# A planner that counts ScalarE's function-table loads and prices scans anew, in a hybrid encoder step on one core

## The chip, the cores and the metric

The kernel runs on one core of one Trainium2 chip. The metric is the device time of one execution in microseconds (us), the median of several runs. The engines are named as the profile names them: PE is TensorE's matmul, PEld its weight load, DVE is VectorE, ACT is ScalarE, POOL is GpSimd, SP is SyncE, which issues all DMA transfers here.

## What is computed

One layer of a streaming encoder, for a prompt of 2048 frames and for 32 frames of a running stream with 1024 cached positions. The reference, cut to what matters:

```python
xn = rmsnorm(x, g_mix)                       # model width 1024
q, k, v, u, gate = split(xn @ w_in)          # 5 x 512 columns
q, k = head_rmsnorm(q), head_rmsnorm(k)      # 8 heads of 64
# stick-breaking attention, s < t only:
z = q @ k.T / 8
sp = where(mask, softplus(z), 0)
log_a = log_sigmoid(z) - (reverse_cumsum(sp) - sp)
o = where(mask, exp(log_a), 0) @ v
# convolution branch
c = causal_dwconv(u * sigmoid(gate), 31 taps)
c = silu(layernorm(c))
h = x + concat([o, c]) @ w_out
up = causal_dwconv(rmsnorm(h) @ w_up, 3 taps)    # 5632 columns
a, g = split(up)
y = h + (silu(g) * a) @ w_down
```

## The kernel before

All matrix products run in a split form: a value is kept as a high and a low part (the helper split, line 579: an ACT copy makes the high part, a DVE subtraction the low one), and each product is three matmuls. Phase 1 (line 851) makes the projections of w_in in two halves of the prompt. Then four feed-forward blocks of 512 frames follow (feed, line 1213): for each of 22 column tiles two up projections of 24 matmuls and more, an ACT eviction, three DVE steps of the short convolution, one Silu on ACT over the gate's tile (inside up, line 1238), a product and a split; every second tile the down projection of a pair is added, behind the next tile's up projections. Two generators are woven between these steps (weave, line 1384): attention (attend, line 914), the output projections with their Silu (conv_out, line 1090), and the depthwise convolution of 31 taps, which is DVE work (conv, line 590). Attention(0) and (1) run in the second half of phase 1; the 32 running frames (sample_pair, line 979) in block 0; attention(2) and (3) in blocks 1 and 2. Block 3 has nothing woven in.

Attention needs no exponentials. ACT makes the survival probability 1 - sigmoid(z) as Sigmoid with scale -0.125, out of a PSUM bank; DVE turns it into a running product along reversed columns with one scan; the scan of the next 512 keys starts from the last column of this one (carry). PE transposes the result, split makes its two parts, and PE multiplies them with the differences of the values. So four scans and four Sigmoids belong to 512 queries by 512 keys of one head.

No engine's order is written out by hand. The helpers mm, tr, act, vec, pool and dma do not emit instructions; they add steps to a list (Plan.add, line 194) with an engine, an expected duration and the memory that is read and written. A matmul joins the step before it if it writes the same bank, up to 8 in a step. Plan.run (line 236) then plays the list through: each engine has a heap of ready steps, `now`, ordered by rank. The rank is the place of a step in the program as written, raised to that of anything it depends on. When an engine is free, the ready step of least rank is taken, its end is the time plus its expected duration, and what depends on it becomes ready after a fixed latency between the two engines. The PSUM banks (8) are given out in the same pass. The order that results for each engine is fixed in the program; on the chip every engine goes through its own in that order and waits by semaphores.

A Sigmoid and a Silu need different function tables on ACT. Copy, Identity and Square, the other functions here, run under either. The compiler puts an instruction ACT_TABLE_LOAD ahead of an activation whose table is not the loaded one; it appears in the profile under line 438, that of the helper act, with no tile's name. In the kernel before, the planner does not know of it: act's expected duration (line 435) is a constant plus the width, the same for all functions. Line 463 to 465 (vec_price) has the price of DVE steps, scans among them:

```python
return n * 2.1 + 50 if name == "tensor_tensor_scan" else n / 0.96 + 68 + 61 * pointers
```

In the profile all matmuls stand under line 424, transposes under 431, ACT under 438, DVE and POOL under 453, DMA issues under 482, since those are the lines of the helpers. "arena" and "arena_r" are two large SBUF tensors in which every tile has a place; "arena_r" holds the operands of matmuls. An ACT row arena<-bank is a Sigmoid or an eviction, arena<-arena is a Silu of the gate (or work of a norm, where it has 1024 columns), arena_r<-bank or arena_r<-arena is the high part of a split.

Of the kernel before, what the change touches and what calls it, by code (L numbers as in the profile page):

```python
# [13 lines left out]
AF = mybir.ActivationFunctionType  # L14
# [126 lines left out]

LATE = 0

LAST_SIDE = FT - 3


class Plan:
# [10 lines left out]
    def __init__(self, tc, banks):  # L158
        self.tc, self.banks = tc, banks
        self.n_banks = 0  # L160
        self.uses = {}
        self.steps = []
        self.writers, self.readers = {}, {}
        self.former, self.keys = {}, {}
        self.late = 0

    def bank(self):

        self.n_banks += 1
        return bass.AP(self.banks[0].tensor, (self.n_banks - 1) * BANK, self.banks[0].ap)  # L170
# [20 lines left out]
        grain = self.GRAIN if ap.ap[0][0] * size > 2048 else 8  # L191
        return [(name, g) for g in range(lo * size // grain, (hi * size + size - 1) // grain + 1)]

    def add(self, engine, ns, call, writes, reads, gets=(), puts=()):
        i = len(self.steps)
        last = self.steps[-1] if self.steps else None
        out = writes[0].offset // BANK if engine == "pe" else None
        if out is not None and last and last[0] == "pe" and last[5] == out and len(last[2]) < 8:
            i -= 1
            last[1] += ns  # L200
            last[2].append(call)
        else:
            last = [engine, ns, [call], set(), i + self.late, out]
            self.steps.append(last)
        waits = last[3]
        for ap in (*reads, *writes):
            if ap.space == PSUM:
                uses = self.uses.setdefault(ap.offset // BANK, [])
                if i not in uses:
                    uses.append(i)  # L210
        for ap in reads:
            for g in self.grains(ap):
                waits.update(self.writers.get(g, ()))
                if ap.space == PSUM:

                    waits.update(self.readers.get(g, ()))
                self.readers.setdefault(g, set()).add(i)
        for ap in writes:
            for g in self.grains(ap):
                before = self.readers.pop(g, None)  # L220
                w = self.writers.get(g, ())
                if engine == "sp" and w and not before and all(self.steps[j][0] == "sp" for j in w):

                    self.writers[g] = [*w, i]
                    waits.update(self.former.get(g, ()))
                    continue
                self.former[g] = {*(before or ()), *w}
                waits.update(self.former[g])
                self.writers[g] = [i]
        for k in gets:  # L230
            waits.update(self.keys[k])
        for k in puts:
            self.keys.setdefault(k, []).append(i)
        waits.discard(i)

    def run(self):
        steps = self.steps
        n = len(steps)
# [7 lines left out]
        now = {e: [] for e in engines}  # L246
# [43 lines left out]
        def pick():  # L290

            for x in shut[:1]:
                if fits(x[2]):
                    return x
            for x in shut:
                if place[x[2]] == oldest:
                    return x
            return None

        for i in range(n):  # L300
            if not left[i]:
                heapq.heappush(soon[steps[i][0]], (0.0, rank[i], i))
        done = 0
        while done < n:

            t, e = None, None
            for x in engines:
                y = None
                if now[x]:
                    y = free[x]  # L310
                elif soon[x]:
                    y = max(free[x], soon[x][0][0])
                if x == "pe" and idle and pick():
                    z = max(free[x], idle[0][0])
                    y = z if y is None else min(y, z)
                if y is not None and (t is None or y < t):
                    t, e = y, x
            while soon[e] and soon[e][0][0] <= t:
                _, r, i = heapq.heappop(soon[e])
                if i in opens:  # L320
                    heapq.heappush(shut, (r, i, opens[i]))
                else:
                    heapq.heappush(now[e], (r, i))
            if e == "pe" and idle and idle[0][0] <= t:
                take = pick()
                if take and not (now[e] and now[e][0] < take[:2]):
                    shut.remove(take)
                    heapq.heapify(shut)
                    heapq.heappush(now[e], take[:2])
                    self.home[take[2]] = heapq.heappop(idle)[1]  # L330
                    open_.add(take[2])
                    while oldest < len(turn) and turn[oldest] in self.home:
                        oldest += 1
            if not now[e]:
                continue
            done += 1
            r, i = heapq.heappop(now[e])
            ns = steps[i][1]
            start[i] = t
            if e == "sp":  # L340
                dge = max(t + 80, dge) + 470
                dma = max(dge + 660, dma) + ns
                free[e], end = t + 60, dma
            else:
                free[e] = end = t + ns
            for k in closes.get(i, ()):
                left_in[k] -= 1
                if not left_in[k]:
                    open_.discard(k)
                    heapq.heappush(idle, (end + LATENCY[e]["pe"], self.home[k]))  # L350
            for j in then[i]:
                when[j] = max(when[j], end + LATENCY[e].get(steps[j][0], 1000))
                left[j] -= 1
                if not left[j]:
                    heapq.heappush(soon[steps[j][0]], (when[j], rank[j], j))
# [16 lines left out]
def hybrid_step_kernel(  # L372
# [33 lines left out]
    nc = tc.nc  # L406
    psum = ctx.enter_context(tc.tile_pool(name="psum", bufs=1, space=PSUM))
    plan = Plan(tc, [psum.tile([P, 512], F32, name=f"bank{i}")[:] for i in range(8)])

    def width(ap):  # L410
        n = 1
        for d in ap.shape[1:]:
            n *= d
        return n

    def aps(*xs):
        return [x for x in xs if isinstance(x, bass.AP)]
# [16 lines left out]
    def act(out, in_, func, **kw):  # L434
        ns = width(in_) / 1.2 + (51 if in_.space == PSUM else 94) + 93 * len(aps(*kw.values()))
        reads = aps(in_, kw.get("scale"), kw.get("bias"))
        plan.add(
            "act", ns, lambda: nc.scalar.activation(out, plan.real(in_), func, **kw), aps(out, kw.get("accum_out")), reads  # L438
        )

    class Engine:
# [20 lines left out]

    def vec_price(name, n, pointers):

        return n * 2.1 + 50 if name == "tensor_tensor_scan" else n / 0.96 + 68 + 61 * pointers

    vec = Engine("dve", nc.vector, vec_price)
    pool = Engine("pool", nc.gpsimd, pool_price)

# [9 lines left out]
    def dma(dst, src, gets=(), puts=()):  # L479
        dst, src = (x.bitcast(F32) if x.dtype == F32R else x for x in (dst, src))  # L480
        ns = dst.size() * 4 / 360 * (1 if min(run(dst), run(src)) >= 128 else 2)
        plan.add("sp", ns, lambda: nc.sync.dma_start(dst, src), [dst], [src], gets, puts)  # L482
# [83 lines left out]
    def columns(dst, rows, n):  # L566
        t = slot("ini", (P,))
        dma(t[:n, :], rows)
        ps = bank()
        tr(ps[:, :n], t[:n, :], ident[:n, :n])  # L570
        act(dst, ps[:, :n], AF.Copy)
# [7 lines left out]
    def split(hi, lo, src):  # L579
        act(hi, src, AF.Copy)  # L580
        vec.tensor_tensor(lo, src, hi.bitcast(F32), ALU.subtract)
# [631 lines left out]
    def feed(b, upto):  # L1213
# [12 lines left out]
        def tick():  # L1226
            done[0] += 1
            if done[0] < total * (LAST_SIDE + 1) / FT:
                upto(done[0] / total * FT / (LAST_SIDE + 1))

# [137 lines left out]
        for f in range(FT):  # L1368
            group.append(up(f))
            if f == LAST_SIDE and b + 1 < NBLK:  # L1370
                upto(1.0)
# [125 lines left out]
```

## Time and profile before

| | us |
|---|---|
| median of 3 runs (2920.81 to 2928.97) | 2927.1 |
| the profiled execution | 2924.49 |
| its span, first to last instruction | 2922.7 |
| PE busy | 2729.2 (93%) |
| DVE busy | 2041.6 (70%) |
| ACT busy | 1147.4 (39%) |
| POOL busy | 395.1 (14%) |

A row of the profile names the line, the engine, the operation, what is written and read, the shape, how often (x), the busy time and the mean duration, and the idle time of the engine ahead of such instructions with what ended it. PE's matmuls are pipelined and their ends are modelled, so a busy PE is not a PE at its peak. The mean granted TensorE clock is 0.977 of full speed. The chain of waits follows the work that ended last back from the end, at each step to what released it; the shares of its parts are shares of the span. A wait for several semaphores is put down to the one that came last.

### The profile page before, as it was taken

Reading aid. Unit: us, or ns where it says so; the run is one execution under the profiler, and the core shown is the slowest. Engines: PE = TensorE matmul, PEld = TensorE weight load, DVE = VectorE, ACT = ScalarE, POOL = GpSimd, SP = SyncE. Lnnn points to the kernel's source line nnn. Section 1 sums busy time; section 2 is a strip of 40 time slices with the busy share of each in tenths; the row PEclk is TensorE's granted clock in tenths of the full one; section 3 lists DMA queues with packets and bytes.
Section 4 is the critical chain, followed back from the end, with each engine's and each line's share of the span. In section 5 each row is a group of like instructions: output and inputs, shape, how many; then the busy total and the mean of one; then the engine's idle time right before and its main releaser. Section 6 shows DMA issues by size and latency. Waiting matters only on the chain.

```text
span 2922.7 us, 42946 instructions
## 1 busy us (share of the span) xinstructions
PE 2729.2 (93%) x16218; PEld 2391.3 (82%) x16218; DVE 2041.6 (70%) x3055; ACT 1147.4 (39%) x2087; POOL 395.1 (14%) x809
## 2 busy tenths in 40 slices
PE   7998999989889999999999999999999979999999
PEld 7988898888767777778888877887777857899998
DVE  3476578679799776658887776779889745444444
ACT  4144434345544444435454454344444423211111
POOL 1144113224111010100000010001011000000000
PEclk9999999999899999999999999999999989999999
DMA  5255546654687998874555547664554466544443
GB/s 168 77 167 161 152 142 190 202 176 130 185 282 260 304 304 263 288 260 163 184 180 177 185 164 219 245 214 156 171 171 158 148 216 215 208 173 173 173 173 133
DMA packets 290696, 563.44 MB, mean 193 GB/s; under 512 B 33810, under 2 KB 175518, under 8 KB 256697
## 3 DMA queue, kind: packets, MB, share of 16 engines
q1 hardware_dynamic: 290489, 560.71, 58.4%
q8 instruction: 127, 2.08, 0.3%
q14 instruction: 80, 0.66, 0.1%
HBM read 410.14 MB, written 146.22 MB: 190 GB/s over the span
## 4 chain that ended last, share of the span: by engine, by line
PE 47%; DVE 13%; DMA 10%; ACT 4%; issue 4%; POOL 2%; SPq 1%; POOLq 0%; DVEq 0%; ACTq 0%
PE bank L424 44%; DVE arena L453 10%; DMA arena_r<-wu_d 4%; PE bank L431 3%; DVE arena_r L453 3%; ACT arena L438 2%; DMA arena<-in_w_up_dram 2%; ACT arena_r L438 1%; SPq L482 1%; ACT L438 1%; DMA h_d<-arena 1%; POOL arena L453 1%; POOL few L453 1%; DMA arena<-oT_d 1%; DMA arena<-in_w_out_dram 0%
## 5 line engine op out<-in xcount | busy, mean ns | idle before, releaser
L424 PE MATMUL bank<-arena_r 128*128 128x512 f32 (+6 forms) x14224 | 2544.8, 338 | 90.0 <-DMA arena_r<-wu_d 26.1
L424 PEld LDWEIGHTS bank<-arena_r 128*128 128x128 f32 x14224 | 2180.4, 192 | 378.8 <-DVE arena_r L453 33.1
L438 ACT ACTIVATE arena<-bank 128x512 f32<-128x512 f32 (+8 forms) x699 | 333.4, 501 | 859.4 <-PE bank L424 654.6
L438 ACT ACTIVATE arena_r<-arena 128x512 fp32r<-128x512 f32 (+2 forms) x428 | 288.4, 682 | 430.0 <-DVE arena L453 95.2
L453 DVE TENSOR_TENSOR arena<-bank,arena 128x512 f32<-128x512 f32 (+3 forms) x488 | 305.8, 635 | 182.5 <-PE bank L424 155.4
L453 DVE TENSOR_TENSOR_SCAN arena<-arena 128x512 f32<-128x512 f32 (+4 forms) x332 | 365.1, 1106 | 66.8 <-ACT arena L438 38.9
L453 DVE SCALAR_TENSOR_TENSOR arena<-arena,wdw 128x512 f32<-128x512 f32 (+1 forms) x600 | 402.0, 670 | 8.0
L453 DVE TENSOR_TENSOR arena_r<-arena,arena_r 128x512 fp32r<-128x512 f32 (+2 forms) x428 | 321.6, 765 | 105.8 <-ACT arena_r L438 103.5
L438 ACT ACTIVATE arena_r<-bank 128x512 fp32r<-128x512 f32 (+1 forms) x388 | 202.4, 562 | 283.0 <-PE bank L431 268.4
L431 PE MATMUL bank<-ident,arena 128*128 128x128 f32 (+5 forms) x1654 | 235.8, 279 | 74.1 <-DVE arena L453 59.6
L453 DVE TENSOR_SCALAR arena<-arena,wfd,bfd 128x512 f32<-128x512 f32 (+1 forms) x176 | 97.5, 554 | 293.6 <-ACT arena L438 293.6
L431 PEld LDWEIGHTS bank<-ident,arena 128*128 128x128 f32 (+5 forms) x1654 | 190.6, 143 | 114.9 <-DVE arena L453 77.8
L453 DVE SCALAR_TENSOR_TENSOR arena<-arena,wfd 128x512 f32<-128x512 f32 (+1 forms) x352 | 265.6, 755 | 8.7 <-DVE arena L453 0.5
L453 POOL COPY halo<-arena 128x2 f32<-128x2 f32 x220 | 55.6, 266 | 1293.0 <-ACT arena L438 1262.5
L453 DVE TENSOR_TENSOR arena_r<-bank,arena_r 128x512 fp32r<-128x512 f32 (+3 forms) x300 | 184.1, 640 | 56.7 <-ACT arena_r L438 55.9
L438 ACT ACT_TABLE_LOAD x107 | 137.3, 1283 | 8.5 <-DVE arena L453 5.5
L438 ACT ACTIVATE arena<-arena 128x512 f32<-128x512 f32 (+3 forms) x122 | 92.1, 756 | 110.3 <-DVE arena L453 97.3
L453 POOL TENSOR_SCALAR_AFFINE_SELECT arena<-arena 128x128 f32<-128x128 f32 x128 | 60.1, 476 | 426.5 <-ACT arena L438 423.7
L453 DVE TENSOR_TENSOR arena<-arena 128x512 f32<-128x512 f32 (+3 forms) x97 | 71.4, 736 | 61.8 <-ACT arena L438 35.0
L453 POOL TENSOR_TENSOR few<-few,nhalf 128x1 f32<-128x1 f32 (+3 forms) x87 | 101.3, 1164 | 7.1
L453 POOL TENSOR_SCALAR few<-few 128x1 f32<-128x1 f32 (+3 forms) x87 | 38.0, 437 | 446.4 <-DVE few L453 307.3
L453 POOL COPY arena<-halo 128x2 f32<-128x2 f32 x176 | 68.7, 391 | 184.6 <-DVE arena L453 177.9
(48 smaller groups left out, 449.9 us busy)
## 6 DMA issues: line engine op xcount, KB each, us to landing
arena_r<-wu_d SPq DMA_DIRECT2D x132, 1024.0 KB
arena_r<-wd_d SPq DMA_DIRECT2D x66, 1024.0 KB
wu_d<-arena_r SPq DMA_DIRECT2D x44, 1024.0 KB
arena<-in_w_up_dram SPq DMA_DIRECT2D x88, 256.0 KB
wd_d<-arena_r SPq DMA_DIRECT2D x22, 1024.0 KB
arena_r<-kT_d SPq DMA_DIRECT2D x80, 256.0 KB
arena_r<-dv_d SPq DMA_DIRECT2D x80, 256.0 KB
arena<-in_w_out_dram SPq DMA_DIRECT2D x80, 256.0 KB
```

What stands on the lines that cost most here:

```text
L424: lambda: nc.tensor.matmul(plan.real(out), lhsT, rhs, start=start, stop=stop),
L431: "pe", in_.shape[0] * (0.4167 if in_.dtype == F32R else 0.8333) + 2.5, lambda: nc.tensor.transpose(plan.real(out), in_, idt), [out], [in_ ...
L438: "act", ns, lambda: nc.scalar.activation(out, plan.real(in_), func, **kw), aps(out, kw.get("accum_out")), reads
L453: self.tag, self.price(name, n / (2 if fast else 1), pointers), lambda: fn(out, *map(plan.real, args), **kw), [out], aps(*args, *kw.values())
L482: plan.add("sp", ns, lambda: nc.sync.dma_start(dst, src), [dst], [src], gets, puts)
```

## The change

The planner gets a notion of ACT's loaded table. Plan.add takes a parameter table, which act sets to the function if that is Sigmoid or Silu. In Plan.run, when the ACT step of least rank needs a table other than the loaded one, the ready ACT steps that need none, or the loaded one, and whose rank is less than 120 above are looked at; the least of them is taken in its stead and the first goes back to the heap. If there is none, the step is taken, its table counts as loaded, and 1290 ns are added to its duration. Beside this the price of a scan goes from 2.1 ns a column plus 50 to 2.2 ns plus 75. Nothing else in the program differs; the steps and their dependencies are the same.

```diff
+TABLE = 1290
+OVER = 120
...
-    def add(self, engine, ns, call, writes, reads, gets=(), puts=()):
+    def add(self, engine, ns, call, writes, reads, gets=(), puts=(), table=None):
...
             last = [engine, ns, [call], set(), i + self.late, out]
             self.steps.append(last)
+            self.tables.append(table)
...
-        done = 0
+        done, table = 0, None
...
             r, i = heapq.heappop(now[e])
             ns = steps[i][1]
+            if e == "act" and self.tables[i] not in (None, table):
+
+                fits_in = [x for x in now[e] if x[0] < r + OVER and self.tables[x[1]] in (None, table)]
+                if fits_in:
+                    x = min(fits_in)
+                    now[e].remove(x)
+                    now[e].append((r, i))
+                    heapq.heapify(now[e])
+                    r, i = x
+                    ns = steps[i][1]
+                else:
+                    table = self.tables[i]
+                    ns += TABLE
             start[i] = t
...
         plan.add(
-            "act", ns, lambda: nc.scalar.activation(out, plan.real(in_), func, **kw), aps(out, kw.get("accum_out")), reads
+            "act",
+            ns,
+            lambda: nc.scalar.activation(out, plan.real(in_), func, **kw),
+            aps(out, kw.get("accum_out")),
+            reads,
+            table=func if func in (AF.Sigmoid, AF.Silu) else None,
         )
...
-        return n * 2.1 + 50 if name == "tensor_tensor_scan" else n / 0.96 + 68 + 61 * pointers
+        return n * 2.2 + 75 if name == "tensor_tensor_scan" else n / 0.96 + 68 + 61 * pointers
```

## Rows read from the trace of the kernel before

**Rows 1.** The page's head: span, then busy time of each engine

```profile
span 2922.7 us, 42946 instructions
...
PE 2729.2 (93%) x16218; PEld 2391.3 (82%) x16218; DVE 2041.6 (70%) x3055; ACT 1147.4 (39%) x2087; POOL 395.1 (14%) x809
```

**Rows 2.** Windows, blocks 0 to 2: busy PE, PEld, DVE, ACT, POOL; clock; DMA

```profile
800.00:1285.00 485.00, 454.75 (x2065) 364.70 (x2063) 367.58 (x573) 212.27 (x343) 55.71 (x123) 0.98 0.85 282
1285.00:1840.00 555.00, 531.19 (x2777) 445.99 (x2774) 419.84 (x577) 260.29 (x439) 44.74 (x126) 0.99 0.57 187
1840.00:2420.00 580.00, 535.69 (x2677) 441.78 (x2677) 467.46 (x754) 235.21 (x390) 54.20 (x127) 0.98 0.54 185
```

**Rows 3.** Chain of waits: blocks 1 and 2 by line; first and last load

```profile
by line: PE bank L424 61.0%; DVE arena L453 8.2%; PE bank L431 7.6%; issue 6.6%; DMA arena_r<-wu_d 4.8%; ACT arena L438 3.2%; ACT L438 2.4%; DMA h_d<-arena 1.7%; DMA arena_r<-kT_d 1.4%; DVE arena_r L453 0.9%; DMA arena<-oT_d 0.9%; POOL aren
...
by line: PE bank L424 48.8%; DVE arena L453 23.1%; PE bank L431 5.3%; DMA arena_r<-wu_d 3.8%; DVE arena_r L453 3.7%; issue 3.7%; ACT L438 2.9%; ACT arena L438 2.7%; ACT arena_r L438 1.7%; DMA arena<-oT_d 1.5%; DMA arena<-in_w_out_dram 1.4%;
...
917.98 0.34 ACT L438
...
2313.28 1.28 ACT L438
```

**Rows 4.** Table loads: whole run (ns, first and last start); up to 800 us

```profile
L438 ACT ACT_TABLE_LOAD  x107: 1283/1283/1283, 0.7 to 2326.8; - x107
...
L438 ACT ACT_TABLE_LOAD x4 | 5.1, 1283 | 0.8 <-PEq L1486 0.7
```

**Rows 5.** PE's waits in blocks 0, 1, 2, 2: total us, times, longest

```profile
PE bank L424 <- ACT arena_r L438: 12.3, 4, 6.5
...
PE bank L431 <- DVE arena L453: 15.7, 14, 4.9
...
PE bank L431 <- DVE arena L453: 12.8, 15, 1.6
PE bank L424 <- ACT arena L438: 6.2, 4, 2.2
```

**Rows 6.** Timeline of ACT: start, duration, instruction, idle time before; hidden load

```profile
2145.60 1.28 ACT L438 ACT_TABLE_LOAD   x1
2150.79 0.63 ACT L438 ACTIVATE arena<-arena 128x512 f32<-128x512 f32 x1 [3.91 <-DVE arena L453]
```

**Rows 7.** Timelines of ACT and PE, block 2: a load that is paid

```profile
2154.56 1.28 ACT L438 ACT_TABLE_LOAD   x1
2155.86 0.60 ACT L438 ACTIVATE arena<-bank 128x512 f32<-128x512 f32 x1
2156.35 0.59 ACT L438 ACTIVATE arena_r<-bank 128x512 fp32r<-128x512 f32 x1
...
2156.51 3.77 PE L424 MATMUL bank<-arena_r 128*128 128x512 f32 x19 [2.22 <-ACT arena L438]
```

**Rows 8.** Timelines of ACT and PE at the end of block 0

```profile
1220.80 1.28 ACT L438 ACT_TABLE_LOAD   x1
...
1223.64 1.28 ACT L438 ACT_TABLE_LOAD   x1
...
1227.18 1.95 PE L424 MATMUL bank<-arena_r 128*128 128x512 f32 x3 [6.53 <-ACT arena_r L438]
```

**Rows 9.** Scans of 512 columns, then DVE's timeline around one

```profile
L453 DVE TENSOR_TENSOR_SCAN arena<-arena 128x512 f32<-128x512 f32 x224 | 288.3, 1288 | 46.1 <-ACT arena L438 38.1 <-POOL arena L453 5.2
...
2158.51 1.28 DVE L453 TENSOR_TENSOR_SCAN arena<-arena 128x512 f32<-128x512 f32 x1
2159.70 0.23 DVE L453 SCALAR_TENSOR_TENSOR arena<-arena,wdw 128x32 f32<-128x32 f32 x1
```

**Rows 10.** ACT's groups by shape: Silus of the gate, blocks 0 to 2

```profile
L438 ACT ACTIVATE arena<-arena 128x512 f32<-128x512 f32 x66 | 41.7, 631 | 34.7 <-DVE arena L453 34.2
```

**Rows 11.** DVE's waits for ACT in block 1: total us, times, longest

```profile
DVE arena L453 <- ACT arena L438: 83.4, 65, 5.4
DVE arena_r L453 <- ACT arena_r L438: 30.9, 32, 3.3
```

More of the change, by code (lines that the diff above doesn't have):

```diff
@@ L165, in __init__ @@
         self.late = 0
+        self.tables = []
     def bank(self):
```

## The prediction

> **What bounds the kernel now.** I read the page's totals first, then the windows by stage, then the chain of waits, and only then ScalarE's own rows. The totals [rows 1] show TensorE (PE) at 93% of the span, VectorE (DVE) at 70%, ScalarE (ACT) at 39%. So ACT's 1147 us of work do not set the time; only where PE stands still because of ACT can a change of ACT's order pay. The profiled execution took 2924.5 us, of which 2922.7 are its span and 1.8 lie around it; the median of the three runs is 2927.1, that is 2.6 us more. I make the sum on the profiled execution and add those 2.6 at the end.
>
> The windows [rows 2] cut the span where the feed-forward blocks begin: block 0 runs from 800 to 1285 us, block 1 to 1840, block 2 to 2420. Attention, the output projections and the depthwise convolution are woven into these three. PE is busy there for 1521.6 of 1620 us, so it is idle for 98 us. What it waits for in them [rows 5] is mostly ACT and DVE: the four largest such rows alone are 12.3, 15.7, 12.8 and 6.2 us, 47 us together. Those four rows, not ACT's share of busy time, are the field that this change plays on.
>
> Next, where the table loads lie. There are 107 of 1283 ns, together 107 x 1.283 = 137.3 us, and all but 4 start after 800 us [rows 4]; after 2326.8 us there are none, since block 3 has Silu alone. I counted by what stands behind each: 54 loads for Sigmoid (attention; the program's first load is among them), 53 for Silu (the gate and conv_out). In 30 of the 107 the next activation had to wait for its input at least until the load had ended; [rows 6] shows such a pair: the load at 2145.60, its Silu 3.9 us after the load's end. Those loads cost nothing. In the other 77 the activation starts 0.01 us after the load [rows 7]: there the load is paid by whoever waits for ACT.
>
> Is anyone on the path waiting? The chain of waits says yes, moderately: line L438 without a tile's name is the table load, and it takes 2.4% of block 1's stretch (13.3 us) and 2.9% of block 2's (16.8 us). Piece by piece the whole chain holds 29 loads, 34.7 us; [rows 3] has the first and the last. Of these, 21 (25.8 us) stand ahead of a Sigmoid and 8 (8.8 us) ahead of a Silu. That 34.7 us is the most that a perfect order could give.
>
> **The change, part by part.** All of it is in the planner; no instruction of the program is added or dropped, except that the number of table loads follows from ACT's new order. Three edits.
>
> *The charge of 1290 ns.* Until now Plan.run believed that a Sigmoid after a Silu starts at once. Measured, a load adds 1.283 us plus 0.01 to 0.02 on either side [rows 7], so 1290 is right to 2% where the load is paid, and too much by up to all of it in the 30 of 107 where the load ran in idle time. Overcharging is harmless for stalls: the chip is then early. What the charge buys: PE's order is fixed by the plan, and a transpose of scan results that the plan holds ready 1.28 us too early stops every matmul behind it. The 47 us of [rows 5] is made of such stops among others; the longest of L431's in blocks 1 and 2 are 4.9 and 1.6 us, the 29 of them average (15.7 + 12.8) / 29 = 0.98 us, about the size of a load. With the right times the plan puts feed-forward matmuls there. Bounds: 0 (all of the waits have other causes) to -34.7 us (every load on the chain gets covered). I take half, -17 us, because the chain's loads are nearly all of the paid kind but several stand in places without other PE work, such as the end of block 0.
>
> *Ready steps first.* When the next ACT step needs a load, any ready step within 120 places that needs none is taken ahead of it. The gain: such a step no longer waits for load and function. [rows 7] has the pattern: at 2154.56 load, at 2155.86 Sigmoid, and only at 2156.35 the split that PE had been waiting for, 2.22 us of idle PE; had the split gone first it would have been ready 1.8 us earlier (2156.35 - 2154.56). In [rows 8] PE stands idle for 6.53 us at the end of block 0, from 1220.65 on, while a load for a Sigmoid (1220.80) and one for a Silu run ahead of the splits that it waits for. A gain of 1.8 plus two loads, 2.6 us, in these two places; I book -4. The loss: the Sigmoid put back starts later by one such step, about 0.62 us. Behind it on ACT stand the next Sigmoids of its head, and on DVE its scan waits. In 20 to 29 of the 54 Sigmoid loads an ACT step stands behind the Sigmoid that runs without having waited (20 are surely splits or copies, 9 more may be Sigmoids), so 20 to 29 put-backs, 12 to 18 us if every one is on the path. Of all loads on the chain there are 21 of 54 ahead of Sigmoids, so I take 0.4 of the middle, +6. A Silu put back is booked at nothing: its product is used only by the down projection of its pair, which feed issues behind the next step's two up projections. That cover is gone only at a block's last pair, where a put-back costs what it lasts, 0.62 us at a time, in three blocks under 2 us.
>
> *Fewer loads?* Hardly. A Silu is put back only while something else is ready at that instant, and ACT is idle for more than half of blocks 1 and 2 (260.3 of 555 us and 235.2 of 580 us busy, [rows 2]). The 66 Silus of 512 columns [rows 10] come 22 to a block of 485 to 580 us, one in 22 to 26 us on average, so two rarely meet. I expect 95 to 107 loads instead of 107, worth nothing by itself beyond what is booked. The Trainium skill, ScalarE: Activation LUTs, section Table sets: the hidden batching unit, says to do all of one set before switching; this deferral waits too briefly to do that, and what it would give if it did is the third rival. The same page, section What ACT_TABLE_LOAD costs, puts a switch at about 2.66 us, a drain of about 1380 ns included. The trace does not agree: load and gaps make 1.3 us. By the page's figure the 29 loads on the chain would be worth an estimated 77 us and the planner would still charge half.
>
> *The price of scans.* For 512 columns it rises from 512 x 2.1 + 50 = 1125 to 512 x 2.2 + 75 = 1201 ns. The trace's mean is 1288, but DVE starts the next instruction 1.19 us after a scan's start [rows 9], so 1201 is what a scan really occupies, and the old price was 76 ns short. Over 224 such scans that is 17 us of DVE's 2042 us. A PE stop behind four scans in a row would shrink by 0.3 us; for the 29 stops of L431 in [rows 5] that gives at most -9 us. Below: a plan that sees DVE fuller may place the convolution's steps differently, in either direction, and no row prices that; I set the same 9 us against it and take -2, nearest to the small error.
>
> Sum: -17 - 4 + 6 - 2 = -17. The first two terms overlap, since the two places of [rows 8] and [rows 7] also stand on the chain, so I take off their 4: -13. 2924.5 - 13 = 2911.5, plus 2.6 is 2914.
>
> What is late next: in block 1 and 2 DVE, which is busy for 467 of 580 us in block 2 [rows 2], and behind it the weights from DRAM. Neither lets PE fall much below its 98 us of idle time here.
>
> **The rivals.** *Slower: the scan chain loses.* In block 1 DVE waits 83.4 us for ACT's arena results (Sigmoid, Silu, evictions) and only 30.9 us for ACT's splits [rows 11]. The edit gives splits the right of way over just the step that DVE waits for more. If the put-backs come at the upper end and all stand on the path, that is +18 us, and it decides once the plan's cover for them (other DVE steps) is used up; with the plan's gain gone too, 2927 + 15 = 2942. For it: the chain's loads stand 21 to 8 ahead of Sigmoids. Against: the plan now sees this delay and gives PE other work.
>
> *No change.* The loads stay about 107, the 30 hidden ones are charged for nothing, and the PE stops that end at one place open at another, as the whole order after the first attention is dealt anew. 2925. For it: PE has 93% already, and the chain takes only 1.2% from loads.
>
> *Batching after all.* If the Silus do collect and loads fall to a few dozen, the chain's 34.7 us go: 2927 - 35 = 2892. Against it stands ACT's idle time.
>
> **How the numbers follow.** Forecast 2914 (its own range 2897 to 2918): 0.47. Slower rival 2942: 0.20. No change: 0.24. Batching 2892: 0.09. About 0.3%, 9 us, is what a measurement of this kernel can tell from no change, so faster is 0.47 + 0.09 = 0.56, same 0.24, slower 0.20. Both signs hold weight, so the range goes from 2890, below most of the batching case, to 2940, into the slower one.
>
> **What the profile will show.** Right: loads between 95 and 107; line L438 without a name below 1.2% of the chain; the L431 waits for DVE in blocks 1 and 2 below 28.5 us together; at a load, the splits ahead of it and not behind. Wrong: DVE's wait for ACT's arena results above 83 us in block 1 with PE idle for DVE grown as well (the slower rival), loads under 70 (batching), or the same waits under other names (no change). The prediction fails most easily in the -17: it is half of a bound, not a measured thing.

## The result

The changed kernel takes 2891.6 us, the median of 4 runs (2887.4 to 2893.6), against 2926.5 us before (median of 4 runs beside it). The ratio is 0.9893, with a 95% interval from 0.9876 to 0.9909: 1.07% or some 31 to 35 us faster. The forecast was 2914, faster; the measured gain is two and a half times the 13 us that it put.

In the profile after, the lines of helpers have moved (424 is 442, 431 is 449, 438 is 458, 453 is 476). The head of the page answers [rows 1]:

```profile
span 2891.6 us, 42927 instructions
...
PE 2715.4 (94%) x16218; PEld 2385.7 (83%) x16218; DVE 2039.6 (71%) x3055; ACT 1145.8 (40%) x2087; POOL 382.1 (13%) x809
```

DVE and ACT have as much to do as before, to 2 us. PE goes through the same 16218 matmuls and transposes with 13.8 us less busy time, and it stands idle (span less busy time) for 176.2 us instead of 193.5. So 17 of the 31 us of span are idle time. Why the busy time fell is not shown: the ends of matmuls are modelled, and the mean granted clock was 0.98 against 0.977. The clock alone does not explain it, since charge_jitter_up below, at 0.977, has 2720.2 us.

The table loads, which answer [rows 4], are as many as they were:

```profile
L458 ACT ACT_TABLE_LOAD  x107: 1283/1283/1283, 0.7 to 2294.2; - x107
```

So the loads were not avoided; what changed is who stands waiting. To compare equal work I cut both spans at the first gate Silu of each feed-forward block, instead of at the fixed times of [rows 2]. Blocks 0, 1 and 2, first before, then after; columns as in [rows 2]:

```profile
807.10:1296.40 489.30, 461.50 (x2091) 370.34 (x2091) 367.54 (x572) 215.27 (x349) 54.20 (x121) 0.98 0.85 283
1296.40:1907.40 611.00, 585.00 (x3019) 491.41 (x3020) 467.39 (x649) 279.49 (x470) 51.03 (x144) 0.99 0.58 192
1907.40:2521.20 613.80, 564.58 (x2835) 464.71 (x2834) 464.31 (x755) 243.70 (x410) 54.45 (x134) 0.97 0.55 184
```

```profile
813.30:1291.70 478.40, 452.60 (x2079) 363.64 (x2078) 361.57 (x569) 211.70 (x344) 50.59 (x119) 0.99 0.86 288
1291.70:1886.50 594.80, 581.30 (x3019) 490.10 (x3018) 467.49 (x647) 279.92 (x471) 48.41 (x144) 0.99 0.59 198
1886.50:2491.80 605.30, 562.89 (x2832) 465.51 (x2831) 465.39 (x758) 242.76 (x410) 50.19 (x134) 0.97 0.56 187
```

Up to block 0 after is 6.2 us later (813.3 against 807.1), and block 0 then takes 10.9 us less. But 16 more matmuls lie ahead of that cut (5469 against 5453), so the two belong together: at the end of block 0 after is 4.7 us ahead. Block 1 takes 16.2 us less, block 2 8.5 us, and what follows takes 399.8 instead of 401.5. Blocks 1 and 2 carry 80 of the 107 loads and hold 24.7 of the 31.1 us of span.

What PE waits for there tells why. Blocks 1 and 2 together, before and after (who waits, for whom, us in total, times, longest):

```profile
PE bank L431 <- DVE arena L453: 28.5, 29, 4.9
PE bank L424 <- DMA arena_r<-wu_d: 18.6, 10, 8.3
```

```profile
PE bank L442 <- DMA arena_r<-wu_d: 18.1, 9, 7.8
PE bank L442 <- ACT arena_r L458: 11.4, 4, 6.7
...
PE bank L449 <- DVE arena L476: 5.8, 8, 1.3
```

The transposes of scan results (L431, now L449) stopped PE for 28.5 us and now for 5.8. The wait for weights from DRAM stays at 18 us and is now the longest; the one for ACT's splits grows from 7.4 to 11.4. All such rows of PE together go from 74.8 to 55.0 us. In the chain of waits of the stretch from 1840 to 2420 us (block 1's breaks off in the profile after) the loads, which took 2.9% of it in [rows 3], are at 0.4%, 2.3 instead of 16.8 us:

```profile
by line: PE bank L442 64.2%; DVE arena L476 15.1%; PE bank L449 5.9%; DMA arena_r<-wu_d 5.0%; DVE arena_r L476 2.8%; DMA arena<-in_w_out_dram 2.3%; ACT arena_r L458 1.3%; issue 1.3%; ACT arena L458 0.8%; DMA arena<-oT_d 0.7%; ACT L458 0.4%;
```

### The profile page after: what moved, and what is told of

Read it like the earlier page. It is cut to its first block, busy times and chain, and to the rows that moved or that the text cites. A ratio compares the mean times of both kernels' runs of the same rounds, so it can differ in the third digit from the quotient of the medians.

```text
span 2891.6 us, 42927 instructions
## 1 busy us (share of the span) xinstructions
PE 2715.4 (94%) x16218; PEld 2385.7 (83%) x16218; DVE 2039.6 (71%) x3055; ACT 1145.8 (40%) x2087; POOL 382.1 (13%) x809
## 5 line engine op out<-in xcount | busy, mean ns | idle before, releaser
L442 PEld LDWEIGHTS bank<-arena_r 128*128 128x128 f32 (+1 forms) x14224 | 2173.4, 191 | 371.7 <-DVE arena_r L476 30.9
L458 ACT ACTIVATE arena<-bank 128x512 f32<-128x512 f32 (+9 forms) x699 | 334.0, 502 | 812.7 <-PE bank L442 625.3
L449 PE MATMUL bank<-ident,arena 128*128 128x128 f32 (+5 forms) x1654 | 233.1, 279 | 63.0 <-DVE arena L476 43.7
L449 PEld LDWEIGHTS bank<-ident,arena 128*128 128x128 f32 (+5 forms) x1654 | 192.0, 143 | 97.9 <-DVE arena L476 52.9
L458 ACT ACT_TABLE_LOAD x107 | 137.3, 1283 | 11.4 <-DVE arena L476 8.1
L476 POOL COPY arena<-halo 128x2 f32<-128x2 f32 x176 | 60.9, 347 | 199.6 <-DVE arena L476 193.8
```

The costliest lines, as they stand in the source:

```text
L442: lambda: nc.tensor.matmul(plan.real(out), lhsT, rhs, start=start, stop=stop),
L449: "pe", in_.shape[0] * (0.4167 if in_.dtype == F32R else 0.8333) + 2.5, lambda: nc.tensor.transpose(plan.real(out), in_, idt), [out], [in_ ...
L476: self.tag, self.price(name, n / (2 if fast else 1), pointers), lambda: fn(out, *map(plan.real, args), **kw), [out], aps(*args, *kw.values())
```

## The experiments

Theory: PE's order is fixed by a plan, and the plan dated scan results too early by the loads it did not know; with the right dates it puts other matmuls there. Rivals: the right of way of ready steps pays; the price of scans pays; any new order moves the time by chance. Each run was timed beside the kernel before on the same chip; the ratio is against that, with its 95% interval.

| run | median us | before us | ratio |
|---|---|---|---|
| after | 2891.6 | 2926.5 | 0.9893 [0.9876, 0.9909] |
| charge_only | 2887.1 | 2920.2 | 0.9881 [0.9854, 0.9907] |
| defer_only | 2920.2 | 2920.2 | 0.9998 [0.9981, 1.0015] |
| scan_only | 2904.0 | 2920.2 | 0.9942 [0.9919, 0.9964] |
| jitter_up | 2910.5 | 2920.2 | 0.9959 [0.9940, 0.9978] |
| jitter_down | 2921.6 | 2918.5 | 1.0007 [0.9990, 1.0024] |
| noload_before | 2876.8 | 2920.5 | 0.9851 [0.9833, 0.9870] |
| noload_after | 2882.0 | 2920.5 | 0.9874 [0.9854, 0.9894] |
| charge_scan | 2891.5 | 2920.5 | 0.9900 [0.9883, 0.9916] |
| charge_defer | 2892.0 | 2920.5 | 0.9899 [0.9882, 0.9916] |
| charge_645 | 2903.9 | 2918.5 | 0.9949 [0.9934, 0.9964] |
| charge_2660 | 2933.7 | 2918.5 | 1.0061 [1.0038, 1.0083] |
| charge_aware | 2889.5 | 2918.5 | 0.9896 [0.9872, 0.9920] |
| charge_jitter_up | 2890.2 | 2922.8 | 0.9892 [0.9872, 0.9912] |
| charge_jitter_dn | 2891.6 | 2922.8 | 0.9898 [0.9876, 0.9919] |
| scan_jitter | 2905.0 | 2922.8 | 0.9948 [0.9928, 0.9969] |
| scan_over | 2910.9 | 2917.7 | 0.9963 [0.9944, 0.9981] |
| after_aware | 2885.6 | 2917.7 | 0.9884 [0.9868, 0.9901] |

**The three edits one by one.** charge_only is after with two constants put back:

```diff
-OVER = 120
+OVER = 0
...
-        return n * 2.2 + 75 if name == "tensor_tensor_scan" else n / 0.96 + 68 + 61 * pointers
+        return n * 2.1 + 50 if name == "tensor_tensor_scan" else n / 0.96 + 68 + 61 * pointers
```

> Before with the 1290 ns charge alone: no step is put ahead, scans priced as before. If the gain comes from a plan that knows the loads, most of the 35 us shows here: 2890 to 2905. If the right of way of ready steps is what pays, 2920 to 2930. If the price of scans is, 2920 to 2930 too. If any new order moves the time by chance, anything from 2895 to 2945.

It came out at 0.9881, 33 us under before: all of the gain, and 3 us below the range given. In its blocks 1 and 2 the stops at transposes are down as in after:

```profile
PE bank L449 <- DVE arena L476: 9.3, 8, 3.4
```

defer_only keeps OVER = 120, with the old price of scans and

```diff
-TABLE = 1290
+TABLE = 0
```

> Before with the right of way of ready steps alone: the planner tracks the loaded table but charges 0 ns, scans priced as before. Plan theory: within 6 us of before, 2920 to 2932, or slower by up to 18 us where Sigmoids are put back. Right-of-way theory: 2895 to 2905. Scan theory: 2920 to 2930. Chance theory: 2895 to 2945.

0.9998: nothing, neither gain nor the loss that the slower rival feared. PE's stops at transposes are nearly all still there:

```profile
PE bank L449 <- DVE arena L476: 24.1, 28, 1.9
```

scan_only is before with the new price of scans (2.2 and 75).

> Before with the new price of scans alone. Plan theory as put in the prediction: 2918 to 2928 (the price is worth 0 to 9 us). Scan theory: 2890 to 2905, because 224 scans of 512 columns were 76 ns short each and stops behind them add up. Chance theory: 2895 to 2945.

0.9942, 16 us faster. That is more than the plan theory allowed for this edit, and 2904.0 lies at the upper end of the scan theory's 2890 to 2905. The stops are 23 instead of 29 and shorter, none above 1.1 us:

```profile
PE bank L431 <- DVE arena L453: 14.1, 23, 1.1
```

**How much is the deal?** Two controls teach the planner next to nothing, but order everything anew. jitter_up, and jitter_down with 67:

```diff
-        return n * 2.1 + 50 if name == "tensor_tensor_scan" else n / 0.96 + 68 + 61 * pointers
+        return n * 2.1 + 50 if name == "tensor_tensor_scan" else n / 0.96 + 69 + 61 * pointers
```

> A control: before, with the fixed part of the price of all DVE steps but scans 69 ns instead of 68. That teaches the planner nothing that matters, but it deals the order anew. If the gain is from better prices or rules, this is within 6 us of before, 2920 to 2932. If the time is a matter of the deal, it lies off by 10 us or more to either side.

> A second control: before with the fixed part of the price of DVE steps 67 ns instead of 68. The first control, 69, came out 12 us below before. If new deals scatter around before: 2905 to 2935, as likely above as below, and PE's waits for DVE in blocks 1 and 2 stay near 36 us. If the old DVE price was too low in general and 69 helped for that: 2920 to 2935.

The first was 0.4% faster, about 10 us, the second even. Whether 69 helps by chance, or because 68 is too low, the two do not tell apart. Either way a change of 1 ns in a price can be worth 10 us here, and a single variant's 10 us proves nothing. But jitter_up did not touch the stops in question; blocks 1 and 2 have the row of before, with the same total and number:

```profile
PE bank L431 <- DVE arena L453: 28.5, 29, 4.7
```

This profiled execution was its slowest, 2923.2 us, so the trace does not show where the 10 us went.

Since a deal can move the time, the charge and the scan price were dealt anew as well: 69 and 67 ns with the charge, 67 with the price.

> The 1290 ns charge alone, with the fixed part of the price of DVE steps 69 ns instead of 68: the same knowledge, another deal. If the charge's 35 us are its own: 2875 to 2897, PE's waits for DVE in blocks 1 and 2 under 22 us as in charge_only (17.6). If a third of them was luck of the deal: 2897 to 2908.

> The 1290 ns charge alone, with 67 ns instead of 68. Same alternatives: 2875 to 2897 if the 35 us belong to the charge, 2897 to 2908 if part of it was the deal.

> The new price of scans alone, with 67 ns instead of 68 for the other DVE steps. If the 16 us of scan_only belong to the price: 2898 to 2910 again. If they were the deal, as the 12 us of jitter_up: 2910 to 2928.

0.9892 and 0.9898 beside 0.9881: the charge's 31 to 33 us are its own. 0.9948 beside 0.9942: the scan price's 15 to 18 us came back as well. PE's idle time over the whole span sorts the profiles in the same way. It is 193.5 us before, and 196.0 and 193.0 in the two controls. With the scan price it is 181.3 and 180.6 us, and with the charge 170.9, 171.4 and 170.6.

**What the loads cost.** In noload_before the order of before is untouched on every engine, but no load is needed between Sigmoid and Silu, since every Silu is computed as a Sigmoid (gate and conv_out values change for it). noload_after has the same edit on after. Two loads are left in each. The activations take as long as before (the group with the gate's Silus 757 against 756 ns).

```diff
-            "act", ns, lambda: nc.scalar.activation(out, plan.real(in_), func, **kw), aps(out, kw.get("accum_out")), reads
+            "act", ns, lambda: nc.scalar.activation(out, plan.real(in_), AF.Sigmoid if func == AF.Silu else func, **kw), aps(out, kw.get("accum_out")), reads
```

> The order of before, unchanged on every engine, but every Silu is computed as a Sigmoid (the gate's and conv_out's values are wrong for it), so that one table serves all and the loads fall from 107 to one or two. Plan theory: the old order is right for a chip without loads, so the 35 us that the charge gained show here too, 2880 to 2895. If the loads were hidden in the old order and the gain had another source: 2912 to 2922.

> The order of after, with every Silu computed as a Sigmoid, so again one table. Plan theory: the new order has already covered the loads, so taking them away gives little, 0 to 10 us under after: 2880 to 2892. If after still pays for them on the path as the chain of before did (34.7 us), 2855 to 2865.

noload_before is 3 us under the plan theory's range. In the old order the loads cost 1 - 0.9851 = 1.49%, 44 us; in the new order 0.9893 - 0.9874 = 0.19%, about 5 us, and by the two intervals (0.17 and 0.20 points to a side, 0.26 together) anything from nothing to 0.45%. Whatever else the edit may do, the same in both runs, would stand in that figure too. So the change takes away 70% or more of what the loads cost without taking away a load. Where they cost it is seen in noload_before's blocks 0, 1 and 2, cut as above:

```profile
808.10:1296.30 488.20, 462.61 (x2099) 370.92 (x2098) 365.82 (x572) 186.57 (x326) 54.31 (x120) 0.98 0.85 283
1296.30:1882.60 586.30, 575.98 (x3019) 487.84 (x3020) 465.67 (x650) 218.99 (x423) 50.08 (x144) 1.00 0.60 201
1882.60:2480.40 597.80, 562.09 (x2836) 466.37 (x2835) 463.15 (x756) 199.19 (x376) 54.26 (x134) 0.97 0.56 189
```

Block 0 is 1.1 us shorter than before, block 1 24.7, block 2 16.0. So the 22 loads of block 0 cost next to nothing, and the 80 of the other two 40.7 us. Of these, 29.2 us are PE's idle time (75.2 against 46.0 in blocks 1 and 2), the rest is its busy time. Its stops at transposes in blocks 1 and 2, beside 5.8 in after and 9.3 in charge_only (and, in the second row, the stop at the end of block 0):

```profile
PE bank L431 <- DVE arena L453: 8.1, 7, 3.2
...
1226.07 1.95 PE L424 MATMUL bank<-arena_r 128*128 128x512 f32 x3 [4.21 <-ACT arena_r L438]
```

**How exact has the charge to be?** charge_only again, with TABLE = 2660 and TABLE = 645:

```diff
-TABLE = 1290
+TABLE = 2660
```

> The charge alone (no right of way, old price of scans), but of 2660 ns, the figure of the Trainium skill's page ScalarE: Activation LUTs for a switch with its drain, instead of 1290. If the figure of the page is what a switch takes here, this fits the chip better than 1290 and lies 5 to 30 us under charge_only (2887). If 1283 ns is what it takes, as the traces show, the plan holds results back 1.4 us too long: 0 to 15 us above charge_only, 2887 to 2902, since being early costs little.

> The charge alone, of half the load, 645 ns. If the gain follows the fit of the plan to the chip, about half of the 33 us is left: 2897 to 2910. If any charge at all, or any new deal, gives it: as charge_only, 2882 to 2892. If the old order's stops need the whole load covered: 2910 to 2920.

By charge the ratios are 1.000 (before), 0.9949 (645), 0.9881 (1290) and 1.0061 (2660). Half the charge gives near half the gain, double the charge costs more than all of it. The expectation for 2660 was missed by far: 15 us above before, not 0 to 15 above charge_only. In its blocks 1 and 2 PE's stops at transposes are at 17.6 us, and DVE waits twice as long for PE as before (64.8 against 30.5 us). The last row is the head of its profile:

```profile
PE bank L449 <- DVE arena L476: 17.6, 21, 3.2
...
DVE arena L476 <- PE bank L442: 64.8, 63, 8.5
...
PE 2740.0 (94%) x16218; PEld 2398.7 (82%) x16218; DVE 2040.5 (70%) x3055; ACT 1140.7 (39%) x2083; POOL 386.9 (13%) x809
```

DVE waits, as would follow if a result dated too late makes PE put off the transposes and what comes behind them. But that is not where the time went: in its span of 2929.6 us PE stands idle for 189.6 us, less than the 193.5 before. Its busy time is longer, 2740.0 against 2729.2 us for as many matmuls, at a mean granted clock of 0.973 against 0.977. The clock was 0.971 to 0.975 in all five executions and 0.975 to 0.981 in the 17 of before beside them. What in this order goes with the lower clock is not shown.

charge_aware charges a load only for what ACT's idle time ahead of it does not cover; after_aware is the same edit on after.

```diff
-                    ns += TABLE
+                    ns += max(0.0, TABLE - (t - free[e]))
```

> The charge alone, but as the chip pays it: the load starts when the activation before it ends, so only the part of 1290 ns that is longer than ScalarE's idle time ahead of the step is added. In after, 26 and more of the 107 loads ran in idle time and were charged all the same. If overcharging is harmless, as the prediction put it: within 6 us of charge_only, 2881 to 2893. If it wastes cover: 2870 to 2881, towards the 2877 that the old order reached without loads.

> After, with the charge reduced by ScalarE's idle time ahead of the step, as in charge_aware. If the three edits and this take away the same stops: 2882 to 2895. If the hidden loads that are charged still cost cover: 2870 to 2882, the best version.

0.9896 beside charge_only's 0.9881, and 0.9884 beside after's 0.9893: no difference that can be measured in either pair. Charging the loads that ran in idle time anyway costs nothing that can be measured.

**Do the parts add?** charge_scan is after with OVER = 0; charge_defer is after with the old price of scans.

> After without the right of way: 1290 ns charge and new price of scans. Plan theory with additive parts: charge alone was 33 us below before, scans alone 16; together 2872 to 2882 if they add, 2885 to 2892 if they take away the same stops. Right of way worth something: this is slower than after by over 6 us.

> After without the new price of scans: charge and right of way. If the price of scans adds to the charge: 2900 to 2907. If both remove the same stops, or the 16 us of the scans alone were the luck of that deal: 2882 to 2893, as the charge alone.

0.9900 and 0.9899, after 0.9893, charge_only 0.9881: with the charge in place neither other edit adds anything. So the scan price's 16 us are not added to the charge's; the row of stops (28.5 us before, 14.1 with the price, 9.3 with the charge) fits with both taking away the same ones.

scan_over asks whether a scan's price has to fit, with 1278 ns for 512 columns instead of 1201:

```diff
-        return n * 2.1 + 50 if name == "tensor_tensor_scan" else n / 0.96 + 68 + 61 * pointers
+        return n * 2.3 + 100 if name == "tensor_tensor_scan" else n / 0.96 + 68 + 61 * pointers
```

> The price of scans alone, 2.3 ns a column and 100, that is 1278 ns for 512 columns, the trace's mean of 1288, instead of 1201, what a scan occupies. If fit counts: above scan_only (2904), 2906 to 2920. If it is only that results of scans are counted on later: at or under scan_only, 2890 to 2904.

0.9963, less gain than with 1201 and in the range for "fit counts", but the intervals overlap. Both later dates for the results help; that 1201 is the better one is not shown.

No version that computes the reference beats after beyond its interval; after_aware (2885.6) and charge_only (2887.1) have the lowest medians.

## Why the prediction was right in kind and wrong in size

**The charge, booked at -17, measured -31 to -33 in three deals.** This is the step that failed: of the 34.7 us of loads on the chain the prediction took half, because several loads stand in places without other PE work, such as the end of block 0. Such places exist, but they weigh little. Without its loads that block is 1.1 us shorter, and its longest stop goes from the 6.53 us of [rows 8] to 4.21 us, so that the two loads there were worth 2.3 us. The 40.7 us lie in blocks 1 and 2, and there the charge found cover for most of them. The planner's own price is even a little short: 1290 was said to be right to 2%, but a load also takes away the overlap of two activations, and puts off a start by 1.4 us (last section).

**The bound of the chain was no bound either.** The prediction took the 34.7 us as the most that a perfect order could give. noload_before shows 44 us, 38 to 49 by its interval. The chain follows one path and counts a load only where it is itself a link. A load that makes a transpose late, after which PE's fixed order sends the lateness on, would stand there under DVE, PE or idle time; that the missing 9 us are of this kind is not shown. The low bound alone does not explain the miss: the 33 us lie under it, and half of 44 would still have been too little. In the same way the prediction held that PE would not fall much below its 98 us of idle time in the windows of [rows 2]; it has 74.5 there in after.

**The mechanism was right.** PE's L431 waits fell, from 28.5 to 5.8 us. That their average of 0.98 us is about the length of a load was no sign of it, since the 29 stops run from 0.2 to 4.9 us and the scan price alone halves them. What bears the mechanism out is that the row is at 8.1 us without the loads and at 9.3 with the charge alone. The 47 us of [rows 5] are not the four largest such rows: PE's wait for DVE's arena_r in block 0, 8.4 us, is larger than the last of them. Nothing in the sum rests on it.

**The right of way, booked at -4 and +6, measured 0.** defer_only 0.9998, and charge_scan, which lacks it, 0.9900 beside after's 0.9893. The -4 stood on two places. The one in [rows 7] was misread: PE starts at 2156.51, 0.05 us after the Sigmoid has ended (2155.86 + 0.60) and before the split has (2156.35 + 0.59). It waited for the Sigmoid, and a split put ahead would have kept it longer. At the end of block 0 ACT in after does have a Silu and four splits ahead of the load for the Sigmoid:

```profile
1218.90 0.61 ACT L458 ACTIVATE arena<-arena 128x512 f32<-128x512 f32 x1
1219.42 2.17 ACT L458 ACTIVATE arena_r<-arena 128x512 fp32r<-128x512 f32 x4
1221.61 1.28 ACT L458 ACT_TABLE_LOAD   x1
```

But charge_only, without any right of way, has the same order there 0.12 us earlier, and defer_only still has a load ahead of that Silu, at 1222.41. So it was the charge that moved it. The +6 for late scans is in no run either. DVE's wait for ACT's arena results in blocks 1 and 2 falls from 152.4 to 117.4 us, so the slower rival's mechanism did not set in. How that rival's +15 follows from its +18 is not said.

**The number of loads**, said to be 95 to 107 and worth nothing by itself: 107 after, and the gain came all the same. Right. The batching rival did not happen, and by noload_after there would have been some 5 us more in it. Its 2892 is the measured time, but by luck: its condition was a few dozen loads, and there are 107. Only its size, the whole of the chain's loads, was nearer than half of them.

**The scan price, booked at -2, measured -15 to -18 alone and 0 beside the charge.** The term was mis-sized by summing what the price puts on a single stop (0.3 us behind four scans, at most 9 us). scan_only shows the stops halved, 28.5 to 14.1 us, with none above 1.1. In the full change the error did not matter, because beside the charge the price adds nothing.

**"Overcharging is harmless"** held for the loads in idle time (charge_aware, after_aware) and fails as a rule: 2660 ns is slower than no charge at all. The Trainium skill's page ScalarE: Activation LUTs, section What ACT_TABLE_LOAD costs, gives that figure for a switch, with the drain. The traces agree with the 1283 ns that it gives for the load and show no drain: 0.01 to 0.02 us lie on either side. The planner with 1290 is 1.8% faster than with the Trainium skill's figure. The measurement decides.

**No change** was the rival that the re-deal stood for. It is real in size, about 10 us in one of two controls, but it does not explain 33 us that return in three deals.

## What to carry to other kernels

Where a planner fixes each engine's order, a cost that it does not know is paid not by the engine that has it but by whoever was promised its result: look in the trace for many short stops on the busiest engine, here 29 of about 1 us. Take the price from the trace, since half of it gave near half the gain and double of it made the kernel slower than none. To learn what such a cost is worth before touching the order, remove the cost and keep the order, as noload_before does; the share of it on the chain of waits was too low here, 34.7 against 44 us.

## What was not expected of the hardware

A load of ACT's function table takes 1.28 us, 107 times out of 107, with 0.01 to 0.02 us on either side where nothing is waited for. It costs a little more than that: without a load between them, and without a wait, an activation starts 0.10 us before the one ahead ends (median; in [rows 7] the split at 2156.35, the Sigmoid's end at 2156.46), and with a load 1.31 us after it. So the load puts off the start by 1.4 us.

A load can run while its own activation still waits for input ([rows 6]): 21 of the 107 before, and 26 in after, are followed by idle time of 0.18 us or more. (The 30 of the prediction include inputs that came within the last 0.1 us of the load.) It is not always so: 7 loads before and 10 in after themselves stood behind 0.3 to 2.6 us of idle time. An engine at 40% busy held the kernel back by 1.5% through these loads alone.
